# Sums of weights and their products one step later, and one list of eight PSUM banks

## The chip, the cores and the metric

The kernel runs on one core of one Trainium2 chip. What is measured is the device time of one execution in microseconds (us); several plain runs give a median, and one more execution is recorded by the hardware profiler. Engines are called PE (TensorE, the matmuls), PEld (its weight loads), DVE (VectorE), ACT (ScalarE), POOL (GpSimd) and SP (SyncE, whose queue issues most of the loads).

## What is computed

One layer of a hybrid trunk: pre-RMSNorm, a chunked gated linear attention, then a squared-ReLU MLP, each added to the residual, and a last RMSNorm. There are 256 tokens of width 2048; the MLP has 8192 hidden units. All of it is in float32.

```python
h = x
h = h + _gla_mixer(_rmsnorm(h, gla_norm[0]), gla_w_in[0], gla_w_gate_up[0], gla_b_gate[0], gla_o_norm[0], gla_w_out[0])
h = h + _sq_relu_mlp(_rmsnorm(h, mlp_norm[0]), mlp_w_up[0], mlp_w_down[0])
return _rmsnorm(h, final_norm)

def _sq_relu_mlp(h, w_up, w_down):
    a = jax.nn.relu(h @ w_up)
    return (a * a) @ w_down
```

The change touches the MLP.

## The kernel before

Precision. Every float32 operand is split in two parts of a shorter type: `hi` is the operand rounded (a cast on ACT), `lo` the remainder, `raw - hi` (a subtraction on DVE). A product takes three matmuls: hi by hi, hi by lo and lo by hi. `parts` (L107 on) makes the two for a tile of weights; `weights` (L118 on) loads a tile of 512 KB on SP's queue and then makes them. The raw tiles have six buffers, `hi` and `lo` five each (`slots`).

Steps. The MLP's hidden units are cut into eight rounds of 1024. An *up step* (`turned_steps`, L167 on) loads one tile of `w_up` and does 24 matmuls of 256 columns into two banks of PSUM. Eight up steps make a tile of 512 hidden units, and `forms` (L672 on) then takes the two banks: relu times a scale on DVE (`su`), the square on ACT, up to five sums and differences of its blocks on DVE, and `hi` and `lo` of the eight blocks (`act`). In a few up steps the parts are written with a gap between the halves of the tile (the argument `even`): in rounds 1 to 7 it is the fourth step of a round.

A *down step* (`down`, L704 on) loads one tile of `w_down` (256 hidden units by 512 columns). A pass is four such steps, on one round `m` and one group `g` of 512 output columns, and adds into four banks, `b16`, `b32`, `b57` and `bx4`. A step is done in one of two ways. The plain way makes the parts of the whole tile (1024 columns) and does eight block products, 24 matmuls. The way *by sums* (`by_sums`, L652) is a Strassen-Winograd scheme of seven block products, 21 matmuls: three take blocks of the tile itself (parts of 768 columns, `w`), four take sums of its blocks. The sums are three additions on DVE into `work` (L736), whose parts (1024 columns, `wu`) are then made like those of a raw tile. 76 of the 120 down steps go by sums: two of four where `g` is 1 and in the round before the last, two in all in the last round, three of four elsewhere.

At the end of a pass the banks are taken: `b32` and `bx4` are added to `h` (`take`, L698), `b16` and `b57` go to `sums[g]` (L758 on ACT the first time, L760 on DVE later); two passes in a row with the same `g` share their banks.

Order. Eighteen up steps are issued first; then one down step and one up step in turn:

```python
for _ in range(KT + 2):
    next(steps)
for _ in down(passes):
    next(steps, None)
```

`down` yields at the end of each step. A scheduler then orders each engine's instructions by its own estimate of time, keeping this order as the priority and every dependence; on the chip each engine works its queue off in that fixed order, and an instruction that waits holds back all behind it. `tc.issue_after` keeps what is issued under it from being placed ahead of the named instruction. Short pieces of other work (`side`) are issued between matmuls by `pump` under such a bound.

PSUM. Eight banks: a pool `acc_p` with six, and a pool `aux_p` with two. In the MLP the down passes and the first up tile take banks of `acc_p`; all later up tiles take the two of `aux_p`, one tile after the other.

Of the kernel before, what the change touches and what calls it, by code (L numbers as in the profile page):

```python
# [27 lines left out]
F32 = mybir.dt.float32  # L28
# [4 lines left out]
P = 128  # L33
T = 256
NT = T // P
# [12 lines left out]
GT = 512  # L48
# [20 lines left out]
def tile_gla_mlp(ctx, tc, x, xt, cols, w_vg, w_in, w_gate, w_out, w_up, w_down, final_norm, out):  # L69
# [5 lines left out]
    wpool = ctx.enter_context(tc.tile_pool(name="wpool", bufs=5))  # L75
    tmp = ctx.enter_context(tc.tile_pool(name="tmp", bufs=2))
    st = ctx.enter_context(tc.tile_pool(name="st", bufs=3))
    acc_p = ctx.enter_context(tc.tile_pool(name="acc_p", bufs=6, space=bass.MemoryType.PSUM))
    aux_p = ctx.enter_context(tc.tile_pool(name="aux_p", bufs=2, space=bass.MemoryType.PSUM))

    def acc_banks(n):
        return [acc_p.tile([P, 512], F32, tag="acc", name="acc") for _ in range(n)]

    def aux_bank():
        return aux_p.tile([P, 512], F32, tag="aux", name="aux")


    side = deque()
# [13 lines left out]
    last_load, last_hi, last_lo = [None], [None], [None]  # L102

    def slots():
        return [wpool.tile([P, SLOT], F32R, tag=i, name=i) for i in ("hi", "lo")]

    def parts(raw, n, to, pieces=None):  # L107

        hi, lo = to
        for s in (slice(*p) for p in pieces or [(0, n)]):  # L110
            last_hi[0] = nc.scalar.copy(hi[:, s], raw[:, s])  # L111
            last_lo[0] = nc.vector.tensor_tensor(lo[:, s], raw[:, s], hi[:, s].bitcast(F32), op=ALU.subtract)  # L112
        return hi, lo
# [148 lines left out]
    cuts = [(0, 512), (512, 768), (768, WMAX)]  # L262
# [84 lines left out]
    acc = natural(plain_x, rows(w_vg, 0, WMAX), WMAX, cuts, ahead=input_tile)  # L347
# [92 lines left out]
    for half in range(2):  # L440
        acc = turned(stream_x, w_in, KEYW + half * GT, even=(0,) if half else (2, 3), acc=None if half else [aux_bank(), aux_bank()])
# [18 lines left out]
    for half in range(2):  # L460
        acc = turned(stream_x, w_in, half * GT, even=())
# [6 lines left out]
    at = big.tile([P, 2, HEADS, 3 * P + 64], F32R, tag="C", name="at")  # L468
# [34 lines left out]
    acc = natural(plain_x, rows(w_in, 3 * KEYW), G, HALF)  # L503
# [53 lines left out]
    acc = natural(row_x, rows(w_in, 4 * KEYW), G, HALF, order=(EVEN[0], 0, EVEN[1], *(kt for kt in range(1, KT) if kt not in EVEN)))  # L557
# [24 lines left out]
    acc = natural(row_x, rows(w_in, 5 * KEYW), G, HALF)  # L582
# [20 lines left out]
    acc = natural(row_o, rows(w_out, 0), G, HALF)  # L603
# [8 lines left out]
    acc = natural(row_o, rows(w_out, G), G, HALF)  # L612
# [27 lines left out]
    S3, S1, S2, S4, A12, A11, A22, A21 = range(8)  # L640
# [11 lines left out]
    def by_sums(m, g, kp):  # L652
# [2 lines left out]
            return (g, kp) in ((1, 0), (1, 2))  # L655
        return kp < (2 if g == 1 or m == ROUNDS - 2 else 3)

    def up():
        for m in range(ROUNDS):
            for q in range(MR // GT):  # L660
                first = m == q == 0
                acc = acc_banks(2) if first else [aux_bank(), aux_bank()]
                even = (6,) if first else (0,) if m == 0 else (3,) if q == 0 else ()
                yield from turned_steps(lambda kt: (hth[:, kt], htl[:, kt]), w_up, m * MR + q * GT, even, acc, 1)
                if m == 0:
                    flush()
                act = big.tile([P, 4 * G + 64], F32R, tag="BC"[q], name="act")[:, OFF:-16]
                acts[m][q] = act = act.rearrange("p (b i f s) -> p b i f s", b=2, i=2, f=8)
                for b in range(2):
                    forms(m, 2 * q + b, acc[b], act[:, b])  # L670

    def forms(m, kp, bank, act):  # L672
        ways = {by_sums(m, g, kp) for g in range(GROUPS)}
        f = work[:, 2].rearrange("p (f s) -> p f s", f=8)
        s = tmp.tile([P, 2, T], F32, tag="t512", name="su", bufs=3)
        nc.vector.scalar_tensor_tensor(  # L676
            s, bank.rearrange("p (i t) -> p i t", i=2), 0.0, r2row.unsqueeze(1).to_broadcast([P, 2, T]),
            op0=ALU.max, op1=ALU.mult,
        )
        nc.scalar.activation(  # L680
            f[:, A12:].rearrange("p (t i) s -> p i t s", t=2), s.rearrange("p i (t s) -> p i t s", t=2), AF.Square
        )
        if True in ways:
            sub = lambda o, x, y: nc.vector.tensor_tensor(o, x, y, op=ALU.subtract)
            sub(f[:, S3 : S1 + 1], f[:, A21:].to_broadcast([P, 2, P]), f[:, A11 : A22 + 1])
            sub(f[:, S2], f[:, A11], f[:, S1])
            sub(f[:, S4], f[:, A12], f[:, S2])
        some = slice(0 if True in ways else A12, 8 if False in ways else A21)
        x = f[:, some].rearrange("p f s -> p (f s)")
        oh, ol = (act[:, i, some].rearrange("p f s -> p (f s)") for i in range(2))  # L690
        nc.scalar.copy(oh, x)
        nc.vector.tensor_tensor(ol, x, oh.bitcast(F32), op=ALU.subtract)
# [4 lines left out]
    def take(bank, t, lo, n):  # L697
        nc.vector.tensor_tensor(h[:, t, lo : lo + n], bank, h[:, t, lo : lo + n], op=ALU.add)  # L698

    left, right = slice(0, T), slice(T, 2 * T)  # L700
# [3 lines left out]
    def down(passes):  # L704

        for n, (m, g) in enumerate(passes):
            if not n or passes[n - 1][1] != g:
                b32, bx4, b16, b57 = acc_banks(4)
            ends = n + 1 == len(passes) or passes[n + 1][1] != g
            for kp in range(KP):  # L710
                last = ends and kp == KP - 1
                at = lambda f: stationary(m, kp, f)

                def product(bank, o, a, w, c):

                    for i, (x, y) in enumerate(((0, 0), (0, 1), (1, 0))):
                        halves(bank[:, o], a[x], w[y][:, c], bank.name not in used, last and i == 2)
                        used.add(bank.name)

                raw = raw_tile()[:, : 2 * GT]  # L720
                c0 = m * MR + 2 * kp * P
                src = w_down[c0 : c0 + 2 * P, g * GT : (g + 1) * GT].rearrange("(i p) c -> p i c", p=P)
                last_load[0] = nc.sync.dma_start(out=raw.rearrange("p (i c) -> p i c", i=2), in_=src)
                if not by_sums(m, g, kp):
                    w = parts(raw, 2 * GT, slots())
                    for i in range(2):
                        for bank, f in ((b32, (A11, A12)), (bx4, (A21, A22))):
                            product(bank, slice(0, GT), at(f[i]), w, slice(i * GT, (i + 1) * GT))
                    yield
                    continue  # L730
                w = parts(raw, 2 * GT, slots(), [(T, 2 * GT)])
                wk = work[:, n_sums[0] % 2]
                n_sums[0] += 1
                u = wk.rearrange("p (f s) -> p f s", f=4)
                raw = raw.rearrange("p (f s) -> p f s", f=4)
                add = lambda o, x, y: nc.vector.tensor_tensor(o, x, y, op=ALU.add)  # L736
                add(u[:, :2], raw[:, :1].to_broadcast([P, 2, T]), raw[:, 1:3])
                add(u[:, 2], u[:, 0], raw[:, 2])
                add(u[:, 3], u[:, 2], raw[:, 3])
                wu = parts(wk, G, slots())  # L740
                block = lambda i: slice(i * T, (i + 1) * T)
                product(b16, left, at(A11), w, block(1))
                product(b32, right, at(A12), w, block(3))
                product(b32, left, at(S4), w, block(2))
                product(b57, left, at(S1), wu, block(0))
                product(b57, right, at(S3), wu, block(1))
                product(b16, right, at(S2), wu, block(2))
                product(bx4, right, at(A22), wu, block(3))
                yield
            if ends:  # L750
                take(b32, 0, g * GT, GT)
                take(bx4, 1, g * GT, GT)

                e = sums[g]
                for dst, bank in ((e[:, 1:3], b16), (e[:, 0::3], b57)):
                    b = bank.rearrange("p (f s) -> p f s", f=2)
                    if g not in begun:
                        nc.scalar.copy(dst, b)  # L758
                    else:
                        nc.vector.tensor_tensor(dst, b, dst, op=ALU.add)  # L760
                begun.add(g)
                if m == ROUNDS - 1 or m == ROUNDS - 2 and g > 1:
                    side.extend(combine(g))
# [34 lines left out]

    side.extend([lambda t=t, c=c: finish(t, 512 * c, 512) for t in range(NT) for c in range(2)])
    cuts = [HALF, [(0, 512), (512, 768), (768, 1024)]]  # L800
    acc = [[aux_bank(), aux_bank()], acc_banks(3)]
    KL = MR // P
    LAST, ROOM = 6, 2
    room = big.tile([P, 2, ROOM, G], F32R, tag="Al", name="room", bufs=1)
# [8 lines left out]
    for kt in range(KL):  # L813
        k = kt - KL + ROOM
# [9 lines left out]
    for t in range(NT):  # L824
# [13 lines left out]
        for on_act, lo, hi in ((0, 0, 512), (1, 1280, 1664), (0, 512, 1024), (1, 1664, 2048), (0, 1024, 1280)):  # L838
            s = hf[:, t, lo:hi]
# [44 lines left out]
```

## Time and profile before

| what | value |
|---|---|
| median of 3 plain runs | 1079.4 us (1079.35 to 1079.61) |
| the profiled execution, its own time | 1084.84 us |
| its span in the profile | 1082.5 us |
| PE busy | 1068.2 us, 99%, 9202 matmuls |
| DVE busy | 831.1 us, 77% |
| ACT busy | 587.9 us, 54% |
| read from HBM | 206.92 MB, 193 GB/s over the span |

The span runs from the first to the last instruction of the program that the profiler recorded; the execution's own time has a little more around it. A PE that is busy is not PE at its peak: matmuls are pipelined, one starts about 115 ns after the other while each is shown with 278 ns, so how fast PE goes is read from start to start. The idle time of an engine is put down to what ended it.

### The profile page before, as it was taken

Reading aid. Unit: us, or ns where it says so; the run is one execution under the profiler, and the core shown is the slowest. Engines: PE = TensorE matmul, PEld = TensorE weight load, DVE = VectorE, ACT = ScalarE, POOL = GpSimd, SP = SyncE. Lnnn points to the kernel's source line nnn. Section 1 sums busy time; section 2 is a strip of 40 time slices with the busy share of each in tenths; the row PEclk is TensorE's granted clock in tenths of the full one; section 3 lists DMA queues with packets and bytes.
Section 4 is the critical chain, followed back from the end, with each engine's and each line's share of the span. In section 5 each row is a group of like instructions: output and inputs, shape, how many; then the busy total and the mean of one; then the engine's idle time right before and its main releaser. Section 6 shows DMA issues by size and latency. Waiting matters only on the chain.

```text
span 1082.5 us, 22093 instructions
## 1 busy us (share of the span) xinstructions
PE 1068.2 (99%) x9202; PEld 1066.8 (99%) x9202; DVE 831.1 (77%) x1144; ACT 587.9 (54%) x723; POOL 12.8 (1%) x39
## 2 busy tenths in 40 slices
PE   9999999999999999999999999999999999999997
PEld 9999999999999999999999999999999999999996
DVE  5777644656546468798899889889989888979886
ACT  6775445545545355664656555636655655545453
POOL 0000000100000000000000000000000000000000
PEclk9999999999999999999999999999999999999999
DMA  9957765555656665665656657666666665666662
GB/s 338 326 159 207 209 195 156 147 166 176 194 178 191 181 175 175 194 196 190 209 173 215 206 179 209 182 209 187 198 194 205 195 188 181 216 196 186 215 204 78
DMA packets 94787, 210.44 MB, mean 194 GB/s; under 512 B 6704, under 2 KB 7600, under 8 KB 94560
## 3 DMA queue, kind: packets, MB, share of 16 engines
q1 hardware_dynamic: 93728, 206.99, 62.5%
q10 hardware_dynamic: 960, 2.05, 0.5%
q8 instruction: 72, 1.18, 0.4%
q14 instruction: 27, 0.22, 0.1%
HBM read 206.92 MB, written 2.10 MB: 193 GB/s over the span
## 4 chain that ended last, share of the span: by engine, by line
PE 83%; DMA 7%; DVE 7%; issue 2%; ACT 0%; SPq 0%; DVEq 0%; POOLq 0%; POOL 0%; ACTq 0%
PE acc L143 45%; PE aux L180 26%; PE acc L180 8%; DMA raw<-in_w_down 5%; DVE lo L112 3%; PE aux L143 2%; DVE lo L132 1%; DVE work L736 1%; DMA raw<-in_w_vg 1%; PE aux L549 1%; DMA zz<-in_xt 1%; DVE h L698 1%; PE aux L477 1%; DVE sums L760 0%; DVE su L676 0%
## 5 line engine op out<-in xcount | busy, mean ns | idle before, releaser
L112 DVE TENSOR_TENSOR lo<-raw,hi 128x768 fp32r<-128x768 f32 (+3 forms) x226 | 251.6, 1114 | 106.5 <-ACT hi L111 106.2
L143 PE MATMUL acc<-hi,act 128*128 128x256 f32 x1816 | 319.4, 278 | 0.0
L111 ACT CAST hi<-raw 128x768 fp32r<-128x768 f32 (+3 forms) x226 | 217.4, 963 | 176.3 <-PE acc L143 137.9
L143 PEld LDWEIGHTS acc<-hi,act 128*128 128x128 f32 x1816 | 269.9, 188 | 0.0
L180 PE MATMUL aux<-hh,hi 128*128 128x256 f32 x960 | 266.5, 278 | 2.8 <-DVE su L676 2.8
L180 PE MATMUL aux<-hh,lo 128*128 128x256 f32 x960 | 266.7, 278 | 0.2 <-DVE lo L132 0.2
L180 PE MATMUL aux<-hl,hi 128*128 128x256 f32 x960 | 266.5, 278 | 0.0
L131 ACT CAST hi<-raw 128x1024 fp32r<-128x1024 f32 x160 | 167.8, 1050 | 128.0 <-PE aux L180 66.3
L143 PE MATMUL acc<-lo,act 128*128 128x256 f32 x908 | 223.0, 278 | 2.2 <-DVE lo L112 2.2
L132 DVE TENSOR_TENSOR lo<-raw,hi 128x1024 fp32r<-128x1024 f32 x160 | 194.9, 1220 | 34.3 <-ACT hi L131 34.1
L180 PEld LDWEIGHTS aux<-hh,hi 128*128 128x128 f32 x960 | 180.1, 188 | 3.2 <-DVE su L676 3.2
L180 PEld LDWEIGHTS aux<-hh,lo 128*128 128x128 f32 x960 | 180.3, 188 | 0.4 <-DVE lo L132 0.4
L180 PEld LDWEIGHTS aux<-hl,hi 128*128 128x128 f32 x960 | 180.2, 188 | 0.0
L143 PEld LDWEIGHTS acc<-lo,act 128*128 128x128 f32 x908 | 157.5, 188 | 2.6 <-DVE lo L112 2.6
L111 ACT CAST hi<-work 128x1024 fp32r<-128x1024 f32 x76 | 79.9, 1051 | 77.9 <-PE aux L180 56.2
L112 DVE TENSOR_TENSOR lo<-work,hi 128x1024 fp32r<-128x1024 f32 x76 | 92.8, 1221 | 23.6 <-ACT hi L111 23.6
L143 PE MATMUL acc<-hi,xA 128*128 128x256 f32 (+1 forms) x736 | 105.3, 280 | 0.0
L143 PEld LDWEIGHTS acc<-hi,xA 128*128 128x128 f32 x736 | 94.5, 189 | 0.1
L736 DVE TENSOR_TENSOR work<-raw 128x512 f32<-128x512 f32 x76 | 52.5, 690 | 48.0 <-DMA raw<-in_w_down 47.7
L736 DVE TENSOR_TENSOR work<-work,raw 128x256 f32<-128x256 f32 x152 | 63.9, 420 | 1.0
L143 PE MATMUL acc<-lo,xA 128*128 128x256 f32 (+1 forms) x368 | 58.6, 279 | 0.1
L143 PEld LDWEIGHTS acc<-lo,xA 128*128 128x128 f32 x368 | 49.8, 188 | 0.3 <-DVE lo L112 0.3
(165 smaller groups left out, 1209.1 us busy)
## 6 DMA issues: line engine op xcount, KB each, us to landing
raw<-in_w_up SPq DMA_DIRECT2D x128, 512.0 KB, 3.8
raw<-in_w_down SPq DMA_DIRECT2D x128, 512.0 KB, 4.3
raw<-in_w_in SPq DMA_DIRECT2D x80, 512.0 KB, 3.7
raw<-in_w_out SPq DMA_DIRECT2D x32, 512.0 KB, 3.6
raw<-in_w_vg SPq DMA_DIRECT2D x14, 520.0 KB, 8.4
h<-in_x SPq DMA_DIRECT2D x4, 512.0 KB, 8.9
zz<-in_xt SPq DMA_DIRECT2D x3, 384.0 KB, 8.0
fb<-in_final_norm ACTq DMA_DIRECT2D x1, 1024.0 KB, 4.8
```

What stands on the lines that cost most here:

```text
L111: last_hi[0] = nc.scalar.copy(hi[:, s], raw[:, s])
L112: last_lo[0] = nc.vector.tensor_tensor(lo[:, s], raw[:, s], hi[:, s].bitcast(F32), op=ALU.subtract)
L131: last_hi[0] = nc.scalar.copy(to[0], dst)
L132: last_lo[0] = nc.vector.tensor_tensor(to[1], dst, to[0].bitcast(F32), op=ALU.subtract)
L143: nc.tensor.matmul(o[:, m], x, w[:, m], start=first and c == 0, stop=last, skip_group_check=True)
L180: nc.tensor.matmul(o, u[:, i, s], m, start=kt == 0 and n == 0 and j % 2 == 0, stop=kt == KT - 1 and n == 2, skip_group_check=True,)
L477: nc.tensor.matmul(o, kab[:, k[0], c0 + c, k[1] : k[1] + P], q(qt[:, c0 + c]), start=c == 0, stop=c == 1)
L549: nc.tensor.transpose(b[:, o + t * P : o + (t + 1) * P], src[:, t, kt * P : (kt + 1) * P], ident)
L698: nc.vector.tensor_tensor(h[:, t, lo : lo + n], bank, h[:, t, lo : lo + n], op=ALU.add)
L736: add = lambda o, x, y: nc.vector.tensor_tensor(o, x, y, op=ALU.add)
```

## The change

Two edits.

In a down step by sums, the three products that need no sums now come first, right behind the parts of the tile; then the step yields, so that the next up step is issued; and only then come the three additions (bound by `issue_after` to stand behind the last remainder made, that of the up step), the parts of the sums, and the four products that take them. The last part of one down step and the first part of the next so lie between two up steps. A plain step is as it was.

The two pools of PSUM become one with eight named banks. Up to the MLP, `acc_banks` and `aux_bank` go round six and two of them as the pools did; in the MLP an up tile takes two and a down pass four from the front of one list, `free`, and they go back to its end when their taking has been issued. The order in which a pass's banks are named and taken becomes `b16`, `b32`, `b57`, `bx4`, as they are written.

```diff
-    acc_p = ctx.enter_context(tc.tile_pool(name="acc_p", bufs=6, space=bass.MemoryType.PSUM))
-    aux_p = ctx.enter_context(tc.tile_pool(name="aux_p", bufs=2, space=bass.MemoryType.PSUM))
+    psum = ctx.enter_context(tc.tile_pool(name="psum", bufs=1, space=bass.MemoryType.PSUM))
+
+    acc_free, aux_free = deque(range(6)), deque([6, 7])
+
+    def psum_bank(i, name="acc"):
+        return psum.tile([P, 512], F32, tag=f"b{i}", name=name)
...
+    free = deque([*acc_free, *aux_free])
+
     def up():
...
-                acc = acc_banks(2) if first else [aux_bank(), aux_bank()]
+                taken = [free.popleft() for _ in range(2)]
+                acc = [psum_bank(i, "up") for i in taken]
...
                 for b in range(2):
                     forms(m, 2 * q + b, acc[b], act[:, b])
+                free.extend(taken)
...
             if not n or passes[n - 1][1] != g:
-                b32, bx4, b16, b57 = acc_banks(4)
+                taken = [free.popleft() for _ in range(4)]
+                b16, b32, b57, bx4 = (psum_bank(i) for i in taken)
...
                 w = parts(raw, 2 * GT, slots(), [(T, 2 * GT)])
+                block = lambda i: slice(i * T, (i + 1) * T)
+                product(b16, left, at(A11), w, block(1))
+                product(b32, right, at(A12), w, block(3))
+                product(b32, left, at(S4), w, block(2))
+                yield
+
                 wk = work[:, n_sums[0] % 2]
...
-                add(u[:, :2], raw[:, :1].to_broadcast([P, 2, T]), raw[:, 1:3])
-                add(u[:, 2], u[:, 0], raw[:, 2])
-                add(u[:, 3], u[:, 2], raw[:, 3])
+                with tc.issue_after(last_lo[0].ins):
+                    add(u[:, :2], raw[:, :1].to_broadcast([P, 2, T]), raw[:, 1:3])
+                    add(u[:, 2], u[:, 0], raw[:, 2])
+                    add(u[:, 3], u[:, 2], raw[:, 3])
                 wu = parts(wk, G, slots())
-                block = lambda i: slice(i * T, (i + 1) * T)
-                product(b16, left, at(A11), w, block(1))
-                product(b32, right, at(A12), w, block(3))
-                product(b32, left, at(S4), w, block(2))
                 product(b57, left, at(S1), wu, block(0))
                 product(b57, right, at(S3), wu, block(1))
                 product(b16, right, at(S2), wu, block(2))
                 product(bx4, right, at(A22), wu, block(3))
-                yield
             if ends:
-                take(b32, 0, g * GT, GT)
-                take(bx4, 1, g * GT, GT)
...
+                for dst, b in ((e[:, 1:3], b16), (None, b32), (e[:, 0::3], b57), (None, bx4)):
+                    if dst is None:
+                        take(b, 0 if b is b32 else 1, g * GT, GT)
+                        continue
...
+                free.extend(taken)
```

More of the change, by code (lines that the diff above doesn't have):

```diff
@@ L77, in tile_gla_mlp @@
     st = ctx.enter_context(tc.tile_pool(name="st", bufs=3))
-    acc_p = ctx.enter_context(tc.tile_pool(name="acc_p", bufs=6, space=bass.MemoryType.PSUM))
-    aux_p = ctx.enter_context(tc.tile_pool(name="aux_p", bufs=2, space=bass.MemoryType.PSUM))
+    psum = ctx.enter_context(tc.tile_pool(name="psum", bufs=1, space=bass.MemoryType.PSUM))
+    acc_free, aux_free = deque(range(6)), deque([6, 7])
+    def psum_bank(i, name="acc"):
+        return psum.tile([P, 512], F32, tag=f"b{i}", name=name)
     def acc_banks(n):
-        return [acc_p.tile([P, 512], F32, tag="acc", name="acc") for _ in range(n)]
+        acc_free.rotate(-n)
+        return [psum_bank(acc_free[k - n]) for k in range(n)]
     def aux_bank():
-        return aux_p.tile([P, 512], F32, tag="aux", name="aux")
+        aux_free.rotate(-1)
+        return psum_bank(aux_free[-1], "aux")
     side = deque()
@@ L748, in down @@
                 product(bx4, right, at(A22), wu, block(3))
-                yield
             if ends:
-                take(b32, 0, g * GT, GT)
-                take(bx4, 1, g * GT, GT)
                 e = sums[g]
-                for dst, bank in ((e[:, 1:3], b16), (e[:, 0::3], b57)):
-                    b = bank.rearrange("p (f s) -> p f s", f=2)
+                for dst, b in ((e[:, 1:3], b16), (None, b32), (e[:, 0::3], b57), (None, bx4)):
+                    if dst is None:
+                        take(b, 0 if b is b32 else 1, g * GT, GT)
+                        continue
+                    b = b.rearrange("p (f s) -> p f s", f=2)
                     if g not in begun:
@@ L800, in tile_gla_mlp @@
     cuts = [HALF, [(0, 512), (512, 768), (768, 1024)]]
-    acc = [[aux_bank(), aux_bank()], acc_banks(3)]
+    acc = [[psum_bank(free.popleft()) for _ in cuts[t]] for t in range(NT)]
     KL = MR // P
```

## The prediction

> **What bounds the kernel now.** I read the page first, then the windows view over the stretch that the change touches, then the waits inside that stretch, the groups of VectorE (DVE) there, and last the timeline of a few steps.
>
> ```profile
> span 1082.5 us, 22093 instructions
> PE 1068.2 (99%) x9202; PEld 1066.8 (99%) x9202; DVE 831.1 (77%) x1144; ACT 587.9 (54%) x723; POOL 12.8 (1%) x39
> ```
>
> TensorE (PE) has hardly a hole, so on the page it looks like the only bound. DVE at 77% is an average over stages. In the MLP I cut the trace into the six rounds whose up and down steps are interleaved (a round is sixteen pairs of a down step and an up step):
>
> ```profile
> 442.80:529.30 86.50, 85.80 (x736) 85.60 (x735) 74.22 (x100) 50.36 (x58) 0.00 (x0) 1.00 0.64 196
> 529.30:612.70 83.40, 83.40 (x737) 83.40 (x736) 75.47 (x103) 48.22 (x54) 0.00 (x0) 1.00 0.64 202
> 612.70:700.10 87.40, 85.87 (x737) 85.68 (x736) 76.74 (x105) 47.57 (x52) 0.00 (x0) 1.00 0.65 194
> 700.10:786.80 86.70, 85.89 (x738) 85.70 (x737) 76.93 (x106) 47.48 (x52) 0.00 (x0) 1.00 0.64 195
> 786.80:870.20 83.40, 83.40 (x737) 83.40 (x737) 76.28 (x105) 47.70 (x52) 0.00 (x0) 1.00 0.66 199
> 870.20:958.80 88.60, 86.42 (x737) 86.02 (x736) 75.55 (x102) 47.20 (x52) 0.00 (x0) 1.00 0.63 194
> 958.80:1024.00 65.20, 65.20 (x556) 65.20 (x555) 56.43 (x78) 32.13 (x34) 0.00 (x0) 1.00 0.64 197
> ```
>
> Columns: length, then busy time and instructions of PE, its weight loads, DVE, ACT, POOL, the granted clock, the DMA share and GB/s. The six rounds take 516.0 us; PE idles in them 5.2 us, and DVE is busy for 455.2 us, 88%. Rounds of the same 737 matmuls take 83.4 or about 87 us at a granted clock of 1.00. The chain of waits shows why:
>
> ```profile
> 526.32 2.84 PE aux L180 x24
> 531.54 2.72 PE aux L180 x24
> ...
> 638.62 2.83 PE aux L180 x24
> ```
>
> 24 matmuls take 2.72 us (113.3 ns each) or 2.83 us (117.9 ns). The slow pitch begins behind a stall of PE (638.62 stands behind the one at 637) and lasts until the load with a gap in the fourth up step of a round (the row at 526.32 is that step; behind it the pitch is fast). A stall so costs its length and then 4.6 ns for every matmul to the next such step. What causes the stalls stands in the waits from 440 to 1024 us:
>
> ```profile
> DVE work L736 <- DMA raw<-in_w_down: 44.8, 41, 3.3
> ...
> DVE lo L112 <- ACT hi L111: 20.2, 22, 2.0
> ...
> DVE lo L132 <- ACT hi L131: 3.9, 5, 1.6
> ...
> PE aux L180 <- DVE su L676: 2.8, 2, 2.0
> PE acc L143 <- DVE lo L112: 2.2, 2, 1.5
> ```
>
> PE waits for DVE alone. And DVE, 88% busy, loses another 44.8 us to the sums of weights (L736): they stand some steps ahead in its queue, where their load has not landed, and everything behind them waits too. DVE with its waits is within a few us of PE: the nearest rival bound.
>
> **The change, part by part.** First what DVE does for one pair, in rows of its timeline (start, duration; [idle before]), and one handover from ACT:
>
> ```profile
> 602.79 1.03 ACT L111 CAST hi<-work 128x1024 fp32r<-128x1024 f32 x1
> ...
> 603.85 1.23 DVE L112 TENSOR_TENSOR lo<-work,hi 128x1024 fp32r<-128x1024 f32 x1 [0.77 <-ACT hi L111]
> ...
> 628.95 0.69 DVE L736 TENSOR_TENSOR work<-raw 128x512 f32<-128x512 f32 x1 [1.62 <-DMA raw<-in_w_down]
> 629.56 0.95 DVE L112 TENSOR_TENSOR lo<-raw,hi 128x768 fp32r<-128x768 f32 x1
> 630.43 0.88 DVE L736 TENSOR_TENSOR work<-work,raw 128x256 f32<-128x256 f32 x2
> 631.22 1.22 DVE L112 TENSOR_TENSOR lo<-work,hi 128x1024 fp32r<-128x1024 f32 x1
> 632.36 1.22 DVE L132 TENSOR_TENSOR lo<-raw,hi 128x1024 fp32r<-128x1024 f32 x1
> ```
>
> From start to start an instruction takes some 0.08 us less than its duration: 0.61, 0.87, 0.79 (two adds), 1.14 and again 1.14 for the up step: 4.55 us of DVE for a pair with sums. PE needs 21 + 24 = 45 matmuls, 5.10 us fast or 5.31 slow. A plain pair is two remainders on DVE, 2.28 us, against 48 matmuls, 5.44 or 5.66.
>
> *The sums one step later.* The adds now come behind the up step's remainder. By then their load has long landed (see the loads, below): the 44.8 us go. But the built order of the changed kernel shows what comes in their place: the three adds stand together, and the remainder of the sums (`lo<-work`) directly behind them in 46 of 76 places; in the other 30 a part of the activation forms or a bank's taking stands between. That remainder needs `hi`, which ACT can only cast once the third add is done. Before, the adds ran a step or more ahead and this wait was small:
>
> ```profile
> L112 DVE TENSOR_TENSOR lo<-work,hi 128x1024 fp32r<-128x1024 f32 x65 | 79.3, 1220 | 12.8 <-ACT hi L111 12.7
> L736 DVE TENSOR_TENSOR work<-work,raw 128x256 f32<-128x256 f32 x130 | 54.6, 420 | 1.0
> L736 DVE TENSOR_TENSOR work<-raw 128x512 f32<-128x512 f32 x65 | 44.9, 691 | 45.0 <-DMA raw<-in_w_down 44.8
> L692 DVE TENSOR_TENSOR act<-work,act 128x896 fp32r<-128x896 f32 (+2 forms) x24 | 23.9, 995 | 0.0
> L698 DVE TENSOR_TENSOR h<-acc,h 128x512 f32<-128x512 f32 x36 | 23.6, 684 | 0.0
> L760 DVE TENSOR_TENSOR sums<-acc,sums 128x512 f32<-128x512 f32 x30 | 20.0, 684 | 0.0
> L684 DVE TENSOR_TENSOR work<-work 128x128 f32<-128x128 f32 (+1 forms) x51 | 16.8, 329 | 0.0
> L676 DVE SCALAR_TENSOR_TENSOR su<-aux,work 128x512 f32<-128x512 f32 x24 | 15.4, 683 | 0.0
> ...
> L111 ACT CAST hi<-work 128x1024 fp32r<-128x1024 f32 x65 | 68.3, 1051 | 58.4 <-PE aux L180 48.5 <-PE acc L143 6.2 <-issue 3.4
> ```
>
> (These are groups of the six rounds, 442.8 to 958.8.) In a bare place DVE waits for the end of the last add (0.08 past its pitch), a handover (602.79 + 1.03 to 603.85: 0.03), the cast (1.05) and a handover back (0.03): 1.19 us. The adds follow each other, each waiting for the end of the one before: 0.11 us more for the first. A pair with sums so takes 4.55 + 0.11 + 1.19 = 5.85 us of DVE's queue, over PE's 5.10 to 5.31. ACT's queue gains a wait too: the sums' cast waits for the adds with the next two casts of raw weights behind it; they run while DVE does the sums' remainder and its own next one (0.83 and 1.05 us behind the cast, against 1.14 + 0.87), so I cost that at nothing; where PE is late in freeing a slot as well, that cover is gone.
>
> *A round.* 65 sums in six rounds are 11 a round, in four passes of four pairs: three heavy ones (three with sums, one plain) and a light one (two and two). The takings (L698, L760: 66 instructions, 43.6 us) and the forms (L692, L684, L676: 99, 56.1 us), less 0.08 each, are 6.4 and 8.0 us a round, 3.6 a pass. Cover: what stands in the 30 places is worth 0.25 (L684), 0.60 (L676) or 0.91 (L692), 16 us over 76, about 0.5 a heavy pass. DVE's queue then needs
>
> - heavy: 3 x 5.85 + 2.28 + 3.6 - 0.5 = 22.9 us, PE 183 matmuls = 20.7 to 21.6;
> - light: 2 x 5.85 + 2 x 2.28 + 3.6 - 0.4 = 19.5 us, PE 186 = 21.1 to 21.9.
>
> So heavy passes go at DVE's pace. In the light one DVE gains some 2 us on PE, of which the five slots of parts let it keep what they hold. If it keeps all, a round is 3 x 22.9 + 19.5 = 88.2; if none, 3 x 22.9 + 21.5 = 90.2. I take 89.3: relus and takings that stand behind the adds wait for PE now and then, as L698's did not before (0.0), so not all is kept. Six rounds: 535.8, against 516.0: **+19.8 us**. The pitch of PE is inside this (it waits for DVE either way).
>
> *Outside the six rounds.* The last rounds have two sums in four pairs or fewer, DVE 8 x 5.85 + 8 x 2.28 + 14.4 = 79.5 a round under PE's 84: nothing. They ran slow before (65.2 us for 556 matmuls), and a stall in their first heavy stretch keeps that; if not, 2.5 us are won.
>
> *The banks.* One list of eight gives a tile of up sums a second pair to change to, so `aux` no longer waits for `su`: at most the 2.8 us above, inside the rounds. A pass takes two idle banks and two of the last pass, first written a step later: no wait, an up step (2.7 us) covers it. The Trainium skill (Perfetto Trace Analysis, Matmul Optimizations) says to make use of all eight PSUM banks for the sake of instruction-level parallelism. By it alone the sum would be a gain of those 2.8 us; the trace has DVE's queue behind four of the five us, and so I don't go by it.
>
> *Loads.* A raw tile is now freed by the last add, an up step later, in SP's queue (POOL does nothing here).
>
> ```profile
> raw<-in_w_down SPq DMA_DIRECT2D x128, 512.0 KB, 4.3
> ```
>
> Six raw buffers are three pairs, some 15 us; less 4.3 to land and one step of 2.7 leaves 8: no cost. Too small a lead would bring the 44.8 back.
>
> **Sum.** The profiled execution took 1084.84 us (span 1082.5); with 19.8 it is 1104.6. The median of the runs, 1079.4, lies 5.4 below the profiled one: 1099.2. Where the plain runs have fewer stalls before, the rise is up to 5.4 larger, since DVE's 89.3 does not depend on it.
>
> **The rivals.**
> - *Faster.* The waits for loads go and ACT's cast is hidden after all, because DVE runs ahead through the light passes and the plain pairs: then PE never stalls, the pitch stays fast, and six rounds are 6 x 83.4 = 500.4, with 2.5 at the end: -18, 1061. For it: 44.8 us is real and DVE needs only 4.55 + 2.28. Against it: 46 bare places, 65/76 of them in the rounds, times 1.19 is 47 us again, and 16 us of partly covered ones on top. It decides where less than half of the waits remain.
> - *Hardly slower.* DVE's queue comes out just under PE's slow pitch: 6 x 737 x 117.9 ns = 521, +5, 1085.
> - *Much slower.* Nothing is covered and nothing kept (ACT late too): 3 x 23.4 + 21.9 = 92.1 a round, +37, 1116.
> - *Nothing moves*: the scheduler leaves the adds early. The built order speaks against it.
>
> **How the numbers follow.** What a measurement of this kernel can tell from no change is about 0.2%, 2 us. Forecast (1089 to 1109) 0.60; hardly slower 0.15; much slower 0.13; faster 0.09; nothing 0.03. The range 1085 to 1112 leaves out the gain, most of the worst case and the no-change case. Faster 0.09, same 0.04 (nothing moves, and the edge of hardly slower), slower 0.87.
>
> **What would show it.** Right: in the profile after, DVE's adds wait for no DMA (under 5 us), `lo<-work` waits 55 to 75 us for ACT's `hi<-work`, that cast waits for the adds, PE has 15 us or more of idle in many short stalls in the rounds, and rounds are 88 to 91 us. Wrong: rounds of 83.4, or `lo<-work` still waiting under 20 us, or PE waiting for loads.

## The result and the profile after

The changed kernel takes 1106.2 us (median, 1105.5 to 1107.0), the kernel before 1079.4: a ratio of 1.0252, 95% interval 1.0234 to 1.0269. It is 26.9 us slower; 19.8 were forecast, 1099.2 us in a range of 1085 to 1112.

The same views as before, of the changed kernel. Its page first:

```profile
span 1104.9 us, 22086 instructions
PE 1083.0 (98%) x9202; PEld 1074.5 (97%) x9202; DVE 836.9 (76%) x1144; ACT 573.9 (52%) x723; POOL 12.8 (1%) x39
```

The page shows next to nothing: the same matmuls, PE and DVE each a point less busy. The waits from 440 to 1045 us (who waited for whom: us in total, times, longest) tell it:

```profile
ACT hi L117 <- DVE work L754: 225.6, 63, 6.0
DVE lo L118 <- ACT hi L117: 66.0, 60, 1.5
...
DVE su L687 <- PE up L186: 10.4, 9, 1.4
...
ACT hi L117 <- PE acc L149: 7.9, 5, 3.2
ACT hi L117 <- PE up L186: 4.8, 2, 2.9
PE acc L149 <- ACT hi L117: 8.0, 23, 0.8
PE acc L149 <- DVE lo L118: 4.1, 7, 0.7
```

(Lines of code moved by a few: L118 is the remainder, L117 the cast, L754 the adds.) The 44.8 us that the adds waited for loads are gone. In their place DVE's remainders wait 66.0 us for ACT's casts, 1.1 us each time, and the casts of the sums wait 225.6 us for the adds. PE no longer waits for `su`; it waits 30 times, 12.1 us in all, for the parts of the sums and of what is queued behind them (the last two lines). The six rounds, by the windows view (length, then busy time and instructions of PE, PEld, DVE, ACT, POOL, clock, DMA share, GB/s):

```profile
441.20:529.40 88.20, 86.90 (x737) 86.00 (x736) 74.00 (x99) 48.63 (x57) 0.00 (x0) 1.00 0.62 191
529.40:618.50 89.10, 87.68 (x739) 86.99 (x738) 75.57 (x103) 46.38 (x53) 0.00 (x0) 1.00 0.61 186
618.50:710.00 91.50, 89.08 (x738) 87.20 (x737) 78.14 (x107) 45.32 (x51) 0.00 (x0) 1.00 0.61 186
710.00:799.10 89.10, 87.30 (x738) 86.20 (x737) 77.00 (x105) 45.22 (x51) 0.00 (x0) 1.00 0.62 189
799.10:890.60 91.50, 88.70 (x737) 86.81 (x736) 78.14 (x107) 45.32 (x51) 0.00 (x0) 1.00 0.60 186
890.60:980.20 89.60, 87.30 (x737) 86.20 (x736) 77.29 (x103) 46.11 (x53) 0.00 (x0) 1.00 0.62 190
980.20:1046.00 65.80, 65.16 (x564) 64.74 (x563) 58.09 (x81) 31.72 (x35) 0.00 (x0) 1.00 0.62 193
```

539.0 us against 516.0: 23.0 us more, and so all of the 22.4 us that separate the two spans (what lies ahead of the rounds is 1.6 shorter, what lies behind 1.0 longer). Every round now takes 88 to 92 us; none is as fast as the two of 83.4. The place in DVE's queue, by its timeline (start, duration, [idle before]), and below it ACT's queue at the same time:

```profile
661.72 0.68 DVE L754 TENSOR_TENSOR work<-raw 128x512 f32<-128x512 f32 x1
662.32 1.08 DVE L703 TENSOR_TENSOR act<-work,act 128x896 fp32r<-128x896 f32 x1
663.32 0.88 DVE L754 TENSOR_TENSOR work<-work,raw 128x256 f32<-128x256 f32 x2
665.37 1.23 DVE L118 TENSOR_TENSOR lo<-work,hi 128x1024 fp32r<-128x1024 f32 x1 [1.17 <-ACT hi L117]
666.51 1.22 DVE L118 TENSOR_TENSOR lo<-raw,hi 128x1024 fp32r<-128x1024 f32 x1
667.64 1.22 DVE L138 TENSOR_TENSOR lo<-raw,hi 128x1024 fp32r<-128x1024 f32 x1
```

```profile
664.29 1.05 ACT L117 CAST hi<-work 128x1024 fp32r<-128x1024 f32 x1 [3.23 <-DVE work L754]
665.24 1.04 ACT L117 CAST hi<-raw 128x1024 fp32r<-128x1024 f32 x1
666.19 1.04 ACT L137 CAST hi<-raw 128x1024 fp32r<-128x1024 f32 x1
```

The last add ends at 664.20, the cast takes 1.05 us, and DVE stands for 1.17 us. Such waits come some 60 times. The two remainders next in its queue could not have filled the time: their casts stand behind the sums' cast in ACT's queue and start at 665.24 and 666.19. In the trace 46 of the 76 remainders of sums stand directly behind the adds, as in the built order; they wait 1.19 us each on the mean, 54.7 us in all, and the other 30 wait 14.2.

### The profile page after: what moved, and what is told of

It is laid out like the page before. It is cut to its first block, busy times and chain, and to the rows that moved or that the text cites. A ratio compares the mean times of both kernels' runs of the same rounds, so it can differ in the third digit from the quotient of the medians.

```text
span 1104.9 us, 22086 instructions
## 1 busy us (share of the span) xinstructions
PE 1083.0 (98%) x9202; PEld 1074.5 (97%) x9202; DVE 836.9 (76%) x1144; ACT 573.9 (52%) x723; POOL 12.8 (1%) x39
## 4 chain that ended last, share of the span: by engine, by line
PE 86%; DVE 7%; issue 2%; ACT 2%; DMA 1%; SPq 0%; ACTq 0%; POOLq 0%; DVEq 0%; POOL 0%
PE acc L149 49%; PE up L186 28%; PE acc L186 6%; PE aux L186 2%; DVE lo L118 2%; ACT hi L117 1%; DVE lo L138 1%; DVE work L754 1%; DVE su L687 1%; DMA raw<-in_w_vg 1%; PE aux L149 1%; DMA zz<-in_xt 1%; PE aux L555 1%; PE aux L483 1%; DVE work L695 0%
## 5 line engine op out<-in xcount | busy, mean ns | idle before, releaser
L149 PE MATMUL acc<-hi,act 128*128 128x256 f32 x1864 | 336.7, 280 | 8.3 <-ACT hi L117 8.0
L118 DVE TENSOR_TENSOR lo<-raw,hi 128x768 fp32r<-128x768 f32 (+3 forms) x226 | 251.1, 1113 | 105.6 <-ACT hi L117 105.0
L149 PEld LDWEIGHTS acc<-hi,act 128*128 128x128 f32 x1864 | 277.7, 188 | 13.8 <-ACT hi L117 13.8
L117 ACT CAST hi<-raw 128x768 fp32r<-128x768 f32 (+3 forms) x226 | 216.3, 960 | 126.4 <-PE acc L149 103.0
L186 PE MATMUL up<-hl,hi 128*128 128x256 f32 x1024 | 281.7, 279 | 0.0
L186 PE MATMUL up<-hh,hi 128*128 128x256 f32 x1024 | 281.3, 279 | 0.0
L186 PE MATMUL up<-hh,lo 128*128 128x256 f32 x1024 | 273.1, 279 | 0.0
L117 ACT CAST hi<-work 128x1024 fp32r<-128x1024 f32 x76 | 79.8, 1050 | 241.8 <-DVE work L754 230.6
L186 PEld LDWEIGHTS up<-hl,hi 128*128 128x128 f32 x1024 | 192.2, 188 | 0.0
L186 PEld LDWEIGHTS up<-hh,hi 128*128 128x128 f32 x1024 | 192.2, 188 | 0.0
L186 PEld LDWEIGHTS up<-hh,lo 128*128 128x128 f32 x1024 | 186.8, 188 | 0.4
L149 PEld LDWEIGHTS acc<-lo,act 128*128 128x128 f32 x932 | 161.2, 188 | 6.4 <-DVE lo L118 6.3
L118 DVE TENSOR_TENSOR lo<-work,hi 128x1024 fp32r<-128x1024 f32 x76 | 93.0, 1224 | 69.0 <-ACT hi L117 69.0
L754 DVE TENSOR_TENSOR work<-work,raw 128x256 f32<-128x256 f32 x152 | 64.0, 421 | 2.8
L754 DVE TENSOR_TENSOR work<-raw 128x512 f32<-128x512 f32 x76 | 52.0, 684 | 0.0
```

The costliest lines, as they stand in the source:

```text
L149: nc.tensor.matmul(o[:, m], x, w[:, m], start=first and c == 0, stop=last, skip_group_check=True)
L186: nc.tensor.matmul(o, u[:, i, s], m, start=kt == 0 and n == 0 and j % 2 == 0, stop=kt == KT - 1 and n == 2, skip_group_check=True,)
```

## The experiments

Theory A: the added time is this wait. It comes from the bound on the adds, which leaves them directly ahead of the remainder that needs their cast. Theory B: sums and products that come a step later are themselves what costs. Theory C: the banks, handed out in another order, hold PE up. Each kernel was timed beside the kernel before on the same chip; ratios are to that one.

**banks_only.** The new banks, and the down step of before:

```diff
-                block = lambda i: slice(i * T, (i + 1) * T)
-                product(b16, left, at(A11), w, block(1))
...
-                yield
-
                 wk = work[:, n_sums[0] % 2]
...
-                with tc.issue_after(last_lo[0].ins):
-                    add(u[:, :2], raw[:, :1].to_broadcast([P, 2, T]), raw[:, 1:3])
+                add(u[:, :2], raw[:, :1].to_broadcast([P, 2, T]), raw[:, 1:3])
...
+                block = lambda i: slice(i * T, (i + 1) * T)
+                product(b16, left, at(A11), w, block(1))
...
                 product(bx4, right, at(A22), wu, block(3))
+                yield
```

> Only the eight banks from one list; the down step as before (adds and all seven products ahead of the yield). Theory A (the added time is DVE waiting, right behind the three adds, for ACT's cast of the sums): 1076 to 1081 us, at most the 2.8 us that aux waited for su are won; lo<-work waits about 13 us for the cast in the rounds, as before, and the adds wait some 45 us for loads. Theory C (the banks, handed out in another order, hold PE up): 1095 us or more. Theory B (sums and products a step later are what costs) says as A here.

1076.1 us, ratio 0.9952 (0.9927 to 0.9976): C falls. The adds wait 55.6 us for loads, some 45 were expected. The banks win about 5 us (2.6 to 7.9 by the interval), more than the 2.8 us of waits that they were to take away. In the profiles, behind 400 us, PE's gaps fall by 5.3 us and the matmuls at the slow pitch from 3186 to 2427, worth 3.5; the profiled execution of before was one of its longer ones.

**sums_only.** The kernel before with the changed down step (and the two pools):

> Only the sums and their products one step later, with the two pools of before. A and B: 1104 to 1108 us, the whole loss, with the same stalls of PE behind hi<-work and lo<-work as in the changed kernel. C: near 1080 us.

1107.7 us, ratio 1.0234 (1.0182 to 1.0286): the whole loss, with the same 66.0 us of DVE waiting for casts. What the banks win by themselves does not show beside it (the changed kernel, with them, has a ratio of 1.0252).

**adds_unbound.** The changed kernel, less the bound on the adds:

```diff
-                with tc.issue_after(last_lo[0].ins):
-                    add(u[:, :2], raw[:, :1].to_broadcast([P, 2, T]), raw[:, 1:3])
-                    add(u[:, 2], u[:, 0], raw[:, 2])
-                    add(u[:, 3], u[:, 2], raw[:, 3])
+                add(u[:, :2], raw[:, :1].to_broadcast([P, 2, T]), raw[:, 1:3])
+                add(u[:, 2], u[:, 0], raw[:, 2])
+                add(u[:, 3], u[:, 2], raw[:, 3])
```

> The changed kernel without the bound on the three adds: they are still written behind the up step, but the scheduler may place them ahead of its remainder, and does (some other DVE work then stands between the adds and lo<-work in 69 places of 76, in the changed kernel in 30). A: the wait of lo<-work falls from 69 us to under 25 us, PE stalls under 3 us, 1060 to 1070 us, faster than before; the adds wait for loads again, some 35 us, without harm. B: the products are as late as in the changed kernel, so 1098 to 1107 us.

1065.1 us, ratio 0.9851 (0.9801 to 0.9900): faster than the kernel before, with the sums as late as in the changed one. B falls. Its waits from 440 to 1045 us:

```profile
ACT hi L117 <- PE up L186: 75.4, 49, 1.6
ACT hi L137 <- PE up L186: 58.8, 39, 1.8
ACT hi L117 <- PE acc L149: 44.6, 46, 2.0
DVE work L754 <- DMA raw<-in_w_down: 30.7, 32, 2.9
...
DVE lo L118 <- ACT hi L117: 7.6, 12, 1.4
```

The casts now wait mostly for PE to free a slot: the parts are ahead of PE as far as their buffers allow, where in the changed kernel the first three of these waits were 4.8, 1.9 and 7.9 us. PE waits for nothing. DVE's queue shows why: between an add and the remainder of its sums stand other remainders, which cover the cast. (Their own casts stand ahead of the sums' cast in ACT's queue here.)

```profile
603.47 0.69 DVE L754 TENSOR_TENSOR work<-raw 128x512 f32<-128x512 f32 x1 [0.23 <-DMA raw<-in_w_down]
604.20 0.42 DVE L754 TENSOR_TENSOR work<-work,raw 128x256 f32<-128x256 f32 x1
604.54 0.95 DVE L118 TENSOR_TENSOR lo<-raw,hi 128x768 fp32r<-128x768 f32 x1
605.41 0.42 DVE L754 TENSOR_TENSOR work<-work,raw 128x256 f32<-128x256 f32 x1
606.09 1.23 DVE L138 TENSOR_TENSOR lo<-raw,hi 128x1024 fp32r<-128x1024 f32 x1 [0.26 <-ACT hi L137]
607.24 1.22 DVE L118 TENSOR_TENSOR lo<-work,hi 128x1024 fp32r<-128x1024 f32 x1
```

**sums_in_halves.** The bound stays; the cast is cut in two, so that the first half needs the first add alone:

```diff
-                wu = parts(wk, G, slots())
+                wu = parts(wk, G, slots(), [(0, 2 * T), (2 * T, G)])
```

> The changed kernel with the parts of the sums made in two halves of 512 columns: the first cast needs the first add alone, so ACT casts it while DVE does the other two adds. 76 more casts and 76 more subtractions, some 0.08 us each, 6 us more of DVE's time. A: the waits of DVE on hi<-work fall from 69 us to under 30 us, PE stalls under 3 us, 1060 to 1072 us. B: the products start as late as before and DVE has more to do, 1106 us or more.

1064.9 us, ratio 0.9842 (0.9795 to 0.9889). The group of the sums' remainders, here and in the changed kernel:

```profile
L118 DVE TENSOR_TENSOR lo<-work,hi 128x512 fp32r<-128x512 f32 x152 | 104.2, 685 | 0.4 <-ACT hi L117 0.3
```

```profile
L118 DVE TENSOR_TENSOR lo<-work,hi 128x1024 fp32r<-128x1024 f32 x76 | 93.0, 1224 | 69.0 <-ACT hi L117 69.0
```

11 us more work for DVE in this group (6 were expected), 69 us less waiting, and the loss is gone with the adds still late and bound. Counted over all remainders from 440 to 1045 us, DVE's waits for casts fall from 67.8 to 26.7 us, as other remainders wait more. ACT's casts of the sums still wait 118.5 us for the adds, and PE, behind 400 us, has no gap between matmuls above 140 ns: that much waiting on ACT does no harm.

**bound_not_late.** As banks_only, with the bound alone put on the adds:

```diff
+                with tc.issue_after(last_lo[0].ins):
                     add(u[:, :2], raw[:, :1].to_broadcast([P, 2, T]), raw[:, 1:3])
```

> The eight banks and the down step as before (all seven products ahead of the yield), with the bound alone put on the three adds, here behind the remainder of their own tile. The sums' products are not late. A (the adds' place in DVE's queue, right ahead of lo<-work, is what costs): lo<-work waits over 50 us for the cast in the rounds, PE stalls 15 us or more, 1095 to 1112 us. B (lateness costs): near 1076, as with the banks alone.

1111.3 us, ratio 1.0275 (1.0250 to 1.0299), with 55.8 us of remainders waiting for casts. The four combinations, all with the new banks:

| | products with their step | products a step later |
|---|---|---|
| adds unbound | 1076.1 | 1065.1 |
| adds bound | 1111.3 | 1106.2 |

The bound costs 35 and 41 us. Lateness wins 11 where the adds are unbound. In the lower row it is 5 by the medians, which the ratios do not tell apart (1.0275 and 1.0252, with intervals that overlap); there the bounds differ too, behind the tile's own remainder on the left and the up step's on the right. The run bound_to_own, below, has the bound of the left one.

**half_bound.** The changed kernel, with the bound on every other set of adds:

```diff
-                with tc.issue_after(last_lo[0].ins):
+                with tc.issue_after(last_lo[0].ins) if n_sums[0] % 2 else ExitStack():
```

> The changed kernel with the bound on every other set of adds. A: half of the bare waits, some 35 us less on DVE, bring its queue under PE's time again; since only what exceeds PE's time is lost, nearly all of the loss goes, 1063 to 1072 us. If each bare wait cost its share of the end, 1085 us.

1068.7 us, ratio 0.9889 (0.9855 to 0.9923). DVE still waits 33.0 us for casts, half of 66.0, and 9% of the loss is left (3.6 of 41.1 us). That fits a wait that costs only by what it takes DVE's queue over PE's time, and not one that costs its share each time.

**bound_to_own.** The adds written ahead of the first three products and bound behind their own tile's remainder, with the products of the sums late:

```diff
                 block = lambda i: slice(i * T, (i + 1) * T)
-                product(b16, left, at(A11), w, block(1))
...
-                yield
-
                 wk = work[:, n_sums[0] % 2]
...
                     add(u[:, 3], u[:, 2], raw[:, 3])
+                product(b16, left, at(A11), w, block(1))
...
+                yield
+
                 wu = parts(wk, G, slots())
```

> The changed kernel with the adds written a step earlier, ahead of the three products, and bound behind the remainder of their own tile instead of the up step's; the parts of the sums and their four products stay late. In the built order lo<-work still stands directly behind the adds in 42 places of 76 (46 in the changed kernel). A (what counts is the place in DVE's queue): most of the loss stays, 1094 to 1103 us, lo<-work waiting 50 to 65 us. If the line at which the adds are written counted: near 1065.

1100.2 us, ratio 1.0179 (1.0140 to 1.0218), the remainders of the sums waiting 62.6 us in all. A line moved in the source changes little (6 of 41 us) if the queue comes out nearly the same. And beside bound_not_late, which has the same bound with the products in time, late products again win 11 us (1111.3 to 1100.2; the intervals of the ratios lie apart).

**unbound_halves.** No bound, and halves:

> Adds unbound and the sums' parts in halves, both at once. Each alone brought PE to no stall and the fast pitch from 443 us on, so there is nothing left for the second to win: 1063 to 1068 us. If DVE's queue still set part of the end, under 1062.

1064.9 us, ratio 0.9852 (0.9807 to 0.9896), the same as either alone. These three are faster than both kernels compared, and none is faster than the others. In none of their profiles has PE, behind 400 us, a gap above 140 ns, and fewer than 120 matmuls are slow: what is left there is PE's own time.

Two runs were for the pitch of PE, on which the prediction's reading of a stall's cost rests. **before_no_gap** is the kernel before without the gap in the fourth up step of rounds 1 to 7:

```diff
-                even = (6,) if first else (0,) if m == 0 else (3,) if q == 0 else ()
+                even = (6,) if first else (0,) if m == 0 else ()
```

> The kernel before without the gap in the fourth up step of rounds 1 to 7. If a stall leaves PE at the slow pitch until such a step: behind the first stall near 467 us all matmuls go at 117.8 ns, some 2400 more than in the profile of before, 11 us longer, 1088 to 1093 us. If the pitch comes back by itself or has to do with something else: 1078 to 1082 us.

1085.9 us, ratio 1.0046 (1.0030 to 1.0062): some 5 us longer, between the two ranges, where 11 were expected. The chain of the profiled execution shows where the slow pitch began:

```profile
543.50 5.65 DMA raw<-in_w_down
551.66 3.10 PE aux L180 x24
555.81 2.83 PE aux L180 x24
```

Up to 551.66 no stall came and the pitch was fast; from there it is slow to the end, 4462 of the matmuls behind 400 us against 3186 in the profile of before. That is 5.9 us. Against it the gaps between matmuls above 140 ns add up to 1.5 us here and to 6.6 there; a slower PE asks less of DVE, which would explain it, but no run separates that from a lucky execution. **unbound_no_gap** is the same edit on adds_unbound:

> The unbound kernel, in which PE never stalls, without the gap in rounds 1 to 7. If the gap only mends the pitch behind a stall: nothing to mend, 1063 to 1066 us. If the fast pitch itself needs the gap now and then: 1075 us or more, with slow matmuls.

1067.9 us, ratio 0.9876 (0.9832 to 0.9921), above the 1063 to 1066 expected: two of the four executions took 1064 to 1065 us, two 1071 to 1073, and one of the latter was profiled. There the pitch is fast without a gap from 409 to 903 us, for 4358 matmuls, then comes one short stall (0.4 us), and the rest, 1338, are slow. So the fast pitch needs no gap. In these two profiles a stall ends it, and without the gap it does not come back; other traces have exceptions (last section).

## Why the prediction was right

- **The bound.** That DVE's queue would pace the rounds, by a wait of 1.19 us in each bare place: measured 1.17 in the place shown and 1.19 on the mean of the 46 bare places. (The split is a little off: the 0.08 to the add's end is no part of the idle time that was measured, and the handover to ACT took 0.11, not 0.03.) 69 us of waiting for the sums' casts were measured in all (forecast 55 to 75), none for loads in the adds. The experiments show the cause: the loss goes with the bound or with the halved cast, and comes with the bound alone.
- **The round.** 89.3 us forecast, 539.0 / 6 = 89.8 measured. The mean lies between 88.2 (DVE keeps all that it gains in a light pass) and 90.2 (nothing), but two rounds took 91.5. DVE waited 13.1 us in the six rounds for PE (10.4 before `su`, 2.7 before takings), 2.2 a round where 1.1 had been allowed for, so that the mean came out this close is in part luck.
- **From the profiled execution to the median.** This is the term that was mis-sized. The profiled execution of before lay 5.4 us above its median, and the sum carried that over; the one of after lies 0.7 above its own (1106.95 and 1106.2). That is 4.7 of the 7.1 us missed; the other 2.3 lie in the profiled executions themselves. The direction was written down (the rise up to 5.4 larger, since DVE's pace does not depend on the luck of the loads), but the value taken left it out. The kernel before ranges from 1077 to 1087 us over all comparisons, the changed kernel, whose adds wait for no load, keeps within 1.5 us in four. That fits, but that the loads make the spread is not shown: in sums_only no add waits for a load either, and four executions spread over 4.7 us.
- **PE's idle time.** 15 us or more in many short stalls was the sign named; the windows, by which the prediction counted 5.2 for before, have 12.0 (539.0 less 527.0 busy), so by them the sign was missed. A matmul's modelled end hides part of a short gap. From start to start, behind 400 us, what the gaps above 140 ns have over 115 ns each is 24.3 us, against 6.6 before, and 4215 matmuls against 3186 go at the slow pitch, 4.6 ns each: 17.8 + 4.7 = 22.5, about the difference of the spans.
- **The banks.** Put at 2.8 us at most, they are worth about 5 by themselves: the wait for `su` was counted, the other gaps that went with it and the slow pitch behind them were not, though the prediction had said itself that a stall costs both. The rule of the Trainium skill (Perfetto Trace Analysis, Matmul Optimizations) had the right sign for the banks alone; the whole change came out slower, by DVE's queue, as the prediction had it. (That DVE's queue stood behind four of PE's five us of waits is not in the rows shown there: these are 2.8 for `su` and 2.2 for `lo`.)
- **The rivals.** *Faster* rested on a covered cast. It is what happens, at 1065 us (1061 forecast), as soon as the bound goes or the cast is halved; it was the built order of the changed kernel that spoke against it, and the order decided. *Much slower* (1116) did not come: of the 76 places 30 had cover, and waited 14.2 us in place of some 36. *Nothing moves* fell with the waits for loads, *hardly slower* (1085) with the 1106.
- **What was not seen:** that the late products by themselves are a gain of about 11 us, unbound (1076.1 to 1065.1) and under the same bound (1111.3 to 1100.2). In the profiles of the first pair nearly all of it is pitch: 2427 slow matmuls become 119, and the gaps, 1.3 us, go.

## What to carry to other kernels

Three instructions that hand over from one engine to a second and back cost the first engine the second's whole time if the first and third stand next to each other in its queue (here 1.19 us for a cast of 1.05); put independent work of that length between them, work whose own input the second engine has made ahead, or cut the middle one so that it starts on the first part. A bound that cures one wait (here for a load) fixes an instruction's neighbours too: read the built order around it before trusting it. An engine that is 88% busy in the rounds that matter has little room for waits, whatever the page shows (77% here): beside the unbound adds, 33 us of waiting for casts cost 3.6 us and twice that 41.

## What the runs showed of the hardware

PE has two pitches at a granted clock of 1.00 for the same 256-column matmuls, 113.3 and 117.9 ns, and which one it goes at depends on the past. Behind most stalls seen here it goes at the slow one, for as long as 522 us (552 to 1075 us in before_no_gap). An up step whose weights lie 16 elements further on in their second half mostly brings the fast one back (not in the changed kernel's round at 529 us, which stayed slow). Neither is a rule. In the changed kernel a row of stalls at 827 to 829 us turned the slow pitch into the fast one, for 10 us, with no such step; in half_bound three short stalls near 909 us left the pitch fast; and in sums_only (428 us) and bound_to_own (630 us) the slow one began with no gap above 140 ns. Why, no run here tells. So the price of a stall, its length and 4.6 ns for each matmul to the next such step, is what most of them cost, and no more than that.

Handing over took 0.03 us from ACT to DVE and 0.11 from DVE to ACT (medians of the 46 bare places), so nearly all of a handover's price is the work in the middle.
